# Seven block products in place of eight for the down-projection of two chunks

## The chip, the cores and the metric

The kernel runs on one core of one Trainium2 chip. The metric is the device time of one execution in microseconds, median of the runs; lower is better. All inputs start in HBM and the output ends there.

## The reference, cut to what matters

One layer of a hybrid block on 2048 tokens of width 1024, all in float32:

```
hn  = rms_norm(x, g_mix_pre);  [u | q | k | v] = hn @ w_in
mix = concat[pool_mixer(u), rms_norm_per_head(stick_breaking_attention(q, k, v))] @ w_out
h   = x + rms_norm(mix, g_mix_post)
m   = square(relu(rms_norm(h, g_mlp_pre) @ w_up)) @ w_down      # w_up 1024x4096, w_down 4096x1024
h   = h + rms_norm(m, g_mlp_post)
out = h + sigmoid(h @ w_ple_gate) * rms_norm(p @ w_ple_proj, g_ple)
```

The change is in `square(relu(...)) @ w_down`, in the sums of weights that it needs, and in constants that set the order of everything.

## The kernel before

**Tiling.** Tokens are taken in four chunks of 512 (`CH`), features in tiles of 128 (`P`). Float32 products are made from two halves: a number is split into a rounded high part and the rest (`split`: ScalarE copies the high part, VectorE subtracts), and `mm3` does three matmuls for each tile product (high by high, high by low, low by high), each 128x128 by 128x512. A `page` is an SBUF tile of 128x1024 float32 (512 KB); there are 53 of them (`PAGES`) for everything that moves, and 8 PSUM banks. Split weights are written to HBM at their first use (`dd["w_down"]`, `dd["w_up"]`, ...) and loaded again from there.

**Stages.** First the embeddings (`ple`), projections and attention of the chunks; the feed-forward of chunks 0 and 1 (`mlp_ups`, `mlp_downs`) is mixed with attention. Then chunks 2 and 3 together: `moving_up` builds seven sums and differences of the activations (28 pages, the tile `xs`), and 16 `up_pair` calls each make two of the 32 row tiles of the up-projection for both chunks from seven block products instead of eight (`block`, Winograd's form of Strassen's scheme), 84 matmuls each. The results, `relu` and square applied, are stored as `dd["m"]`. `gate(0)`, the gate of chunk 0, stands before the pairs. Then 8 calls of `down_pair` do the down-projection: each loads four row tiles of `m`, splits them for both chunks, loads four split weights, and for each chunk and each of 8 output tiles runs 4x3 matmuls into one bank, which is added into a running sum in SBUF (tile `acc`). Last come `mlp_post` for chunks 2 and 3 (sum of squares, norm, residual, store `h2`) and the gates of chunks 1, 2 and 3 (tiles `actg`, `gs`, `geh`), which load `h2` again.

**Order.** Nothing runs as written. Every operation is recorded with a time `plan.t` that only TensorE's work moves on; `deadlines` walks back from the users and gives each operation of the other engines the latest time at which it must run. `order` is a list scheduler with a model of the engines, the DMA queue and the pages, which takes the most urgent operation that is ready and fits; `issue` writes the instructions out in that order. So each engine has one fixed order, and every DMA is issued by SyncE's queue, in one fixed order too. The constants (`T_*`, `R_*`, `G_*`, `NORM_LAG`, `AHEAD`, `LEAD`, `EVICT`) shift the due times.

Of the kernel before, what the change touches and what calls it, by code (L numbers as in the profile page):

```python
# [13 lines left out]
F32 = mybir.dt.float32  # L14
# [19 lines left out]
GD = 4  # L34
# [20 lines left out]
G_OUT = 8  # L55
G_OUT2 = 3
G_OUT3 = 12
NORM_LAG = (34.149, 10.442)
# [76 lines left out]
class Op:  # L135
    __slots__ = ("engine", "dur", "calls", "deps", "outs", "allocs", "bufs", "prio", "seq", "place",
                 "left", "ready", "end")
# [14 lines left out]
MARGIN = 2.0  # L152
LATENCY = {
# [9 lines left out]
EVICT = -0.186  # L163
AHEAD = {'pe': 42.752, 'act': 24.695, 'dve': 39.763, 'pool': 25.085, 'sp': 42.237}
LEAD = {'pe': 3.156, 'act': 0.736, 'dve': 0.004, 'pool': 1.033, 'sp': 1.845}
# [31 lines left out]
class Plan:  # L197
# [3 lines left out]
    def __init__(self, tc, banks, pages):  # L201
# [10 lines left out]
        self.t, self.rate, self.bias = 0.0, 1.0, 0.0  # L212
# [23 lines left out]
    @contextmanager  # L236
    def early(self, lead):
        self.bias -= lead
        yield
        self.bias += lead  # L240

    def cost(self, name, method, out, kw, args):
# [11 lines left out]
        if name == "act":  # L254
            psum = all(a.buf.tag in BANKS for a in src if a.buf.tag)
            return (0.051 if psum else 0.093) + n / 1200.0 + (0.07 if len(out.steps) > 2 else 0.0)
        if name == "dve":
            scalars = any(isinstance(kw.get(k), Ref) for k in ("initial", "scalar"))
            if method == "tensor_tensor_scan":
                return 0.2 + n / 460.0  # L260
            return 0.072 + n / 960.0 + (0.058 if scalars else 0.0)
# [36 lines left out]
    def new(self, name, dur):  # L298
        op = Op()
        op.engine, op.dur, op.calls, op.deps, op.allocs, op.bufs = name, dur, [], set(), [], set()  # L300
        op.prio, op.seq, op.end = self.t + self.bias, None, None
# [25 lines left out]
    def deadlines(self):  # L327
# [5 lines left out]
        for op in reversed(self.ops):  # L333
# [4 lines left out]
            op.prio = min(op.prio, late) if e == "pe" else late  # L338
# [146 lines left out]
class Net:  # L485
# [430 lines left out]
    def mlp_ups(self, gi, acts, w_up, dd, first, tag):  # L916
        ms = [[] for _ in acts]
        for j in range(GF):
            unit = self.weight(w_up[gi * GF + j], dd["w_up"][gi * GF + j], first)
            rl = self.page("rl")  # L920
            for i in range(len(acts)):
# [4 lines left out]
                self.dve.tensor_tensor(out=r, in0=r, in1=r, op=ALU.mult)  # L926
# [4 lines left out]
    def moving(self, k, b11, b12, b21, b22):  # L931

        sub = lambda out, a, b: self.dve.tensor_tensor(out=out, in0=a, in1=b, op=ALU.subtract)
# [19 lines left out]
    def moving_up(self, c, d, rows):  # L953

        got = []
        for k2 in range(2):
            low, high = self.both(c, d, k2, rows), self.both(c, d, k2 + 2, rows)
            for j in range(2):
                got.append(self.moving(k2, low[0][:, j, :], low[1][:, j, :], high[0][:, j, :], high[1][:, j, :]))
# [65 lines left out]
    def up_pair(self, b, xs, w_up, dd):  # L1025
        def square(o, t, r):
            self.act.activation(r, r, AF.Relu)
            self.dve.tensor_tensor(out=r, in0=r, in1=r, op=ALU.mult)
# [5 lines left out]
    def down_pair(self, gi, accs, w_down, dd):  # L1034
        ms = [[], []]
        for j in range(GD):
            t = self.page("mi")
            self.sp.dma_start(out=t, in_=dd["m"][gi * GD + j])
            for i in range(2):
                ms[i].append(self.pair("m", t[:, i, :]))  # L1040
        units = [self.weight(w_down[gi * GD + j], dd["w_down"][gi * GD + j], False) for j in range(GD)]
        for i in range(2):
            for ot in range(NK):
                ps = self.bank("dw")
                cs = slice(ot * P, (ot + 1) * P)
                self.mm3(ps, [(units[j][0][:, cs], units[j][1][:, cs], ms[i][j][:, 0, :], ms[i][j][:, 1, :])
                              for j in range(GD)])
                if gi == 0:
                    if ot % 2 == 0:
                        accs[i].append(self.page("acc"))  # L1050
                    self.act.copy(accs[i][-1][:, ot % 2, :], ps)
                else:
                    a = accs[i][ot // 2][:, ot % 2, :]
                    self.dve.tensor_tensor(out=a, in0=a, in1=ps, op=ALU.add)
# [67 lines left out]
def build(tc, x, xr, p, gains, w_in, w_v, w_pool, w_out, w_up, w_down, w_gate, w_ple, out):  # L1122
    with (
# [22 lines left out]
        dd["m"] = [dram(f"m{f}", [P, 2, CH]) for f in range(NF)]  # L1146
        net.h1 = dd["h1"]
# [134 lines left out]
```

## Time and profile before

| | |
|---|---|
| device time, median of 3 runs | 2620.93 us (2620.6 to 2620.98) |
| the profiled execution: device time, span | 2619.36 us, 2617.6 us |
| TensorE matmul busy, granted clock | 2578.0 us (98%), 0.995 |
| VectorE, ScalarE, GpSimd busy | 1781.9 us (68%), 1070.2 us (41%), 683.4 us (26%) |
| DMA: share of 16 engines on the main queue, bytes, mean rate | 69.2%, 653.71 MB, 250 GB/s |

The span is the stretch from the first to the last instruction; 1.76 us of the profiled execution's time lie around it. Matmul busy time is modelled with overlap, so 98% says that TensorE was seldom without a matmul, not that it ran at its peak. Granted clock 1 is 2.4 GHz, 0.5 is 1.2 GHz.

### The profile page before, as it was taken

To read this page: it belongs to the slowest core of one execution; us is meant where nothing else is said; L and a number is where in the kernel's file an instruction comes from. 1 tells how busy PE (TensorE), PEld (TensorE's weight loads), DVE (VectorE), ACT (ScalarE), POOL (GpSimd) and SP (SyncE) were. 2 spreads that over 40 slices of the span, in tenths; PEclk is the share of its full clock that TensorE was granted. 3 is DMA by queue.
4 is the path that set the end of the run, shared out by engine and by line. 5 is a ranking of instruction groups with operands and counts; after the bars stand their busy time and mean duration, and the time that the engine had idled before them with its cause. 6 is when DMAs were issued, how large, how long until landed. Compare 5 with 4: busy or idle time off the path is not lost. (4 is left out here: it accounts for less than half of the span.)

```text
span 2617.6 us, 33833 instructions
## 1 busy us (share of the span) xinstructions
PE 2578.0 (98%) x12088; PEld 2106.5 (80%) x12088; DVE 1781.9 (68%) x2471; ACT 1070.2 (41%) x1999; POOL 683.4 (26%) x635
## 2 busy tenths in 40 slices
PE   8999999999999999999999999999999999999999
PEld 7888787887888888788888888887788888888877
DVE  7375858879888769997758775289856642334464
ACT  9344546646655456455444442134222331010221
POOL 0033536346533444443443541000000000000000
PEclk9999999999999999999999999999999999999999
DMA  9999787986767748774557546676855573432896
GB/s 390 369 354 341 255 300 262 313 297 231 283 239 258 251 156 340 264 273 165 193 169 265 210 150 252 223 307 246 296 201 186 191 299 137 153 137 98 316 359 260
DMA packets 211977, 653.71 MB, mean 250 GB/s; under 512 B 22752, under 2 KB 39136, under 8 KB 211808
## 3 DMA queue, kind: packets, MB, share of 16 engines
q1 hardware_dynamic: 211808, 651.54, 69.2%
q8 instruction: 96, 1.57, 0.2%
q14 instruction: 73, 0.60, 0.1%
HBM read 457.47 MB, written 193.99 MB: 249 GB/s over the span
## 5 line engine op out<-in xcount | busy, mean ns | idle before, releaser
L279 POOL TENSOR_TENSOR pr<-pr,q 128x511 f32<-128x511 f32 (+4 forms) x512 | 573.3, 1137 | 710.3 <-ACT pr L279 281.2
L279 PE MATMUL dw<-m,wh 128*128 128x512 f32 x2048 | 642.4, 395 | 0.0
L279 PE MATMUL dn<-act,wh 128*128 128x512 f32 x1792 | 577.6, 403 | 0.0
L279 DVE TENSOR_TENSOR_SCAN q<-q,ones 128x512 f32<-128x512 f32 (+1 forms) x320 | 405.7, 1284 | 66.1 <-ACT q L279 65.1
L279 PEld LDWEIGHTS dw<-m,wh 128*128 128x128 f32 x2048 | 375.5, 188 | 72.7 <-issue 0.7
L279 PE MATMUL dw<-m,wl 128*128 128x512 f32 x1024 | 399.7, 390 | 0.0
L279 DVE TENSOR_TENSOR acc<-acc,dw 128x512 f32<-128x512 f32 x352 | 237.7, 682 | 237.8 <-PE dw L279 236.8
L279 PEld LDWEIGHTS dn<-act,wh 128*128 128x128 f32 x1792 | 319.7, 190 | 57.9 <-issue 3.2
L279 PE MATMUL dn<-act,wl 128*128 128x512 f32 x896 | 351.9, 393 | 0.0
L279 POOL TENSOR_TENSOR ms<-ms,mhalf 128x4 f32<-128x4 f32 (+1 forms) x36 | 54.3, 1508 | 1046.9 <-DVE ms L279 1013.9
L279 ACT ACTIVATE q<-z 128x512 f32<-128x512 f32 (+1 forms) x320 | 173.2, 542 | 179.6 <-PE z L279 158.6
L279 ACT CAST at<-tp 128x512 fp32r<-128x512 f32 (+2 forms) x320 | 167.5, 530 | 186.6 <-PE tp L279 164.5
L279 PEld LDWEIGHTS dw<-m,wl 128*128 128x128 f32 x1024 | 192.2, 188 | 41.4
L279 DVE TENSOR_TENSOR at<-tp,at 128x512 fp32r<-128x512 f32 (+2 forms) x320 | 189.2, 597 | 48.7 <-ACT at L279 48.1
L279 PEld LDWEIGHTS dn<-act,wl 128*128 128x128 f32 x896 | 168.8, 188 | 37.4
L279 PE MATMUL op<-at,kv 128*128 128x512 f32 (+3 forms) x640 | 185.1, 369 | 8.0 <-DVE at L279 7.8
L279 PE MATMUL dn<-xs,so 128*128 128x512 f32 x768 | 191.8, 389 | 0.0
L279 PE MATMUL z<-kv,qd 128*128 128x512 f32 (+3 forms) x640 | 180.3, 366 | 4.3 <-DVE at L279 3.4
L279 ACT ACTIVATE pr<-z 128x512 f32<-128x512 f32 (+1 forms) x320 | 172.6, 541 | 5.9 <-POOL pr L279 3.1
L279 PE MATMUL tp<-ident,pr 128*128 128x128 f32 x1088 | 170.1, 272 | 2.1 <-DVE acc L279 1.3
L279 PEld LDWEIGHTS dn<-xs,so 128*128 128x128 f32 x768 | 144.1, 188 | 30.5 <-DVE so L279 0.5
L279 PEld LDWEIGHTS tp<-ident,pr 128*128 128x128 f32 x1088 | 135.6, 140 | 40.1 <-DVE acc L279 2.1
(145 smaller groups left out, 3611.0 us busy)
## 6 DMA issues: line engine op xcount, KB each, us to landing
ws<-in_w_up SPq DMA_DIRECT2D x64, 512.0 KB, 5.8
wh<-d_w_down SPq DMA_DIRECT2D x64, 512.0 KB, 5.7
wl<-d_w_down SPq DMA_DIRECT2D x64, 512.0 KB, 5.9
xin<-d_h SPq DMA_DIRECT2D x48, 512.0 KB, 8.3
wh<-d_w_up SPq DMA_DIRECT2D x48, 512.0 KB, 5.3
wl<-d_w_up SPq DMA_DIRECT2D x48, 512.0 KB, 5.5
kv<-d_k SPq DMA_DIRECT2D x80, 256.0 KB, 6.0
kv<-d_v SPq DMA_DIRECT2D x80, 256.0 KB, 6.3
```

The lines of the kernel that those rows point to most:

```text
L279: fn(*[a.real() if isinstance(a, Ref) else a for a in args], **{k: a.real() if isinstance(a, Ref) else a for k, a in kw.items()})
```

## The change

- **Down-projection.** `down_pair` now treats the four row tiles of a group as two pairs, each a 2x2 block problem (two halves of the inner dimension; two halves of the output blocks; two chunks). Per pair it makes four differences of `m` on **GpSimd** (`moving` takes the engine as an argument) and seven splits; three weight halves come from `dd["w_down"]`, four sums of weights from a new store `dd["sd"]`. Seven products times four output blocks, 2x3 matmuls each, go to one bank each and are added into **28 half pages of running sums, one for each product and block, over all 8 groups**. In the last group the loops are turned (output block outside, products inside), and after each block seven additions combine the sums into the outputs of both chunks.
- **Sums of weights.** `stationary_down` runs 16 times, once after each `up_pair`: it loads two raw row tiles of `w_down`, makes four sums on VectorE, splits them, and stores four pages in `dd["sd"]`. `within(SOON)` sets its due time to 15 us after the pair.
- **Squares.** In `mlp_ups` and `up_pair` the square after `relu` moves from VectorE (a product) to ScalarE (`Square`).
- **Rows early.** `prenorm` of chunks 2 and 3 is recorded inside the projection of the chunk before, at a time set back by `T_AHEAD`.
- **Planner.** Durations of ScalarE and VectorE are taken 1.1 times longer (`WEAR`); about twenty constants change, among them the pace of attention (`R_ATT`, `R_ATT2`) and the groups at which the output projections start.

The core of the diff:

```diff
-T_PRE = (12.427, 22.281)
-T_PLE = (0.0, 23.664, 52.404, 38.46)
+T_PRE = (5.628, 28.649)
+T_PLE = (0.0, 23.664, 43.677, 40.12)
-R_ATT = 3.117
+R_ATT = 3.632
+R_ATT2 = 3.024
+T_AHEAD = 30.179
-G_OUT = 8
-G_OUT2 = 3
-G_OUT3 = 12
-NORM_LAG = (34.149, 10.442)
+G_OUT = 4
+G_OUT2 = 1
+G_OUT3 = 11
+NORM_LAG = (39.625, 9.401)
+SOON = 15.0
+WEAR = 1.1
...
-EVICT = -0.186
-AHEAD = {'pe': 42.752, 'act': 24.695, 'dve': 39.763, 'pool': 25.085, 'sp': 42.237}
+EVICT = -0.384
+AHEAD = {'pe': 71.988, 'act': 28.302, 'dve': 36.362, 'pool': 22.185, 'sp': 42.237}
...
                 r = rl[:, i, :]
                 self.act.activation(r, ps, AF.Relu)
-                self.dve.tensor_tensor(out=r, in0=r, in1=r, op=ALU.mult)
+                self.act.activation(r, r, AF.Square)
...
+    def stationary_down(self, n, w_down, dd):
+        f = 4 * (n // 2) + n % 2
+        view = []
+        for i in (f, f + 2):
+            t = self.plan.tile([P, D], F32, "ws")
+            self.sp.dma_start(out=t, in_=w_down[i])
+            v = t.rearrange("p (b h c) -> p h b c", b=4, h=2)
+            view += [v[:, 0], v[:, 1]]
...
+        add(s1[1], a21, a22, ALU.add)
+        add(s2[1], s1[1], a11, ALU.subtract)
+        add(s3[1], a11, a21, ALU.subtract)
+        add(s4[1], a12, s2[1], ALU.subtract)
+        for d, t in zip(dd["sd"][n], (s4, s1, s2, s3)):
+            self.sp.dma_start(out=d, in_=self.pair("so", t[0]).as_(F32))
+
+    def down_pair(self, gi, accs, dd):
+        xs, ws = [], []
+        for j in range(2):
+            low, high = [self.page("mi") for _ in range(2)]
+            for t, f in ((low, 4 * gi + j), (high, 4 * gi + 2 + j)):
+                self.sp.dma_start(out=t, in_=dd["m"][f])
+            xs.append(self.moving(self.pool, low[:, 0, :], low[:, 1, :], high[:, 0, :], high[:, 1, :]))
+            kept = []
+            for f, h in ((4 * gi + j, 0), (4 * gi + 2 + j, 0), (4 * gi + 2 + j, 1)):
+                t = self.page("wa", F32R)
+                for part in range(2):
+                    d = dd["w_down"][f][part].rearrange("p (b h c) -> p h b c", b=4, h=2)[:, h]
+                    self.sp.dma_start(out=t[:, part, :].rearrange("p (b c) -> p b c", b=4).as_(F32), in_=d)
+                kept.append(t)
+            sums = []
+            for i in range(4):
+                t = self.page("wa", F32R)
+                self.sp.dma_start(out=t.as_(F32), in_=dd["sd"][2 * gi + j][i])
+                sums.append(t)
+            ws.append([kept[0], kept[1], sums[0], kept[2], sums[1], sums[2], sums[3]])
+        order = (0, 1, 2, 6, 4, 5, 3)
+        last = gi == NF // 4 - 1
+        steps = [(i, ob) for ob in range(4) for i in order] if last else [(i, ob) for i in order for ob in range(4)]
+        for i, ob in steps:
+            ps = self.bank("dw")
+            cs = slice(ob * P, (ob + 1) * P)
+            self.mm3(ps, [(ws[j][i][:, 0, cs], ws[j][i][:, 1, cs], xs[j][i][:, 0, :], xs[j][i][:, 1, :])
+                          for j in range(2)])
+            a = accs(i, ob)
+            if gi == 0:
+                self.act.copy(a, ps)
+            else:
+                self.dve.tensor_tensor(out=a, in0=a, in1=ps, op=ALU.add)
+            if last and i == order[-1]:
+                for into, of in ((1, 0), (5, 0), (6, 5), (5, 4), (4, 6), (2, 5), (3, 6)):
+                    self.dve.tensor_tensor(out=accs(into, ob), in0=accs(into, ob), in1=accs(of, ob), op=ALU.add)
...
         def project(c):
-            if c > 1:
-                acts[c] = net.prenorm(x[c], xr[c], G_PRE)
             net.in_proj(c, w_in, w_v, acts[c], dd)
+            if 0 < c < NCH - 1:
+                with plan.resumed(plan.t - T_AHEAD):
+                    acts[c + 1] = net.prenorm(x[c + 1], xr[c + 1], G_PRE)
             net.u_proj(c, w_in, acts[c], dd)
...
         for b in range(NF // 2):
             net.up_pair(b, xs, w_up, dd)
-        accs = [[], []]
-        for gi in range(NF // GD):
-            net.down_pair(gi, accs, w_down, dd)
+            with plan.within(SOON):
+                net.stationary_down(b, w_down, dd)
...
+        for gi in range(NF // 4):
+            net.down_pair(gi, sums, dd)
+        accs = [[held[c, ob] for ob in range(4)] for c in (2, 3)]
         net.mlp_post(2, accs[0], dd)
         net.mlp_post(3, accs[1], dd)
```

## Rows read from the trace of the kernel before

**Rows 1.** The page: span and busy time of each engine.

```profile
span 2617.6 us, 33833 instructions
...
PE 2578.0 (98%) x12088; PEld 2106.5 (80%) x12088; DVE 1781.9 (68%) x2471; ACT 1070.2 (41%) x1999; POOL 683.4 (26%) x635
```

**Rows 2.** Windows: bounds, length, busy (x) of PE, PEld, DVE, ACT, POOL, clock, DMA.

```profile
262.00:300.00 38.00, 31.63 (x145) 23.77 (x144) 35.76 (x56) 24.44 (x54) 22.60 (x16) 0.87 0.67 219
...
600.00:680.00 80.00, 74.42 (x359) 59.13 (x357) 75.73 (x81) 54.80 (x101) 51.68 (x38) 0.98 0.79 277
680.00:1766.00 1086.00, 1082.15 (x5238) 885.13 (x5238) 820.89 (x1048) 503.00 (x926) 403.66 (x359) 1.00 0.65 233
1766.00:1857.00 91.00, 86.29 (x376) 70.15 (x375) 85.25 (x138) 33.45 (x59) 1.40 (x1) 0.98 0.68 251
1857.00:2105.00 248.00, 248.00 (x1096) 205.43 (x1095) 162.79 (x261) 69.49 (x122) 0.00 (x0) 1.00 0.57 210
2124.40:2471.40 347.00, 347.00 (x1532) 287.43 (x1531) 127.25 (x196) 52.60 (x95) 0.00 (x0) 1.00 0.48 177
...
2516.00:2534.00 18.00, 15.23 (x56) 11.01 (x55) 14.81 (x24) 5.92 (x11) 0.00 (x0) 0.91 1.02 404
2534.00:2617.60 83.60, 77.67 (x343) 64.02 (x341) 41.54 (x64) 13.91 (x24) 0.00 (x0) 0.99 0.75 286
```

**Rows 3.** The tile dw in the down-projection of chunks 2 and 3.

```profile
L279 PE MATMUL dw<-m,wh x1024: 389/389/389, 2123.2 to 2472.3; 128*128 128x512 f32 x171
...
L279 PE MATMUL dw<-m,wl x512: 389/389/389, 2123.7 to 2472.5; 128*128 128x512 f32 x171
```

**Rows 4.** VectorE's groups over the span, count | busy us, mean ns.

```profile
L279 DVE TENSOR_TENSOR acc<-acc,dw 128x512 f32<-128x512 f32 x352 | 237.7, 682 | 237.8 <-PE dw L279 236.8
...
L279 DVE TENSOR_TENSOR rl<-rl 128x512 f32<-128x512 f32 x64 | 50.6, 790 | 52.7 <-ACT rl L279 52.5
L279 DVE TENSOR_TENSOR so<-sa,so 128x512 fp32r<-128x512 f32 x64 | 44.0, 689 | 8.5 <-ACT so L279 8.0
L279 DVE TENSOR_TENSOR mo<-mo 128x512 f32<-128x512 f32 x64 | 43.8, 689 | 6.9 <-ACT mo L279 6.8
...
L279 DVE SCALAR_TENSOR_TENSOR acc<-acc,gains,nrm 128x512 f32<-128x512 f32 x32 | 22.2, 749 | 3.5 <-ACT nrm L279 3.4
...
L279 DVE TENSOR_TENSOR xin<-xin,acc 128x512 f32<-128x512 f32 x32 | 20.4, 687 | 0.0
...
L279 DVE TENSOR_TENSOR ypool<-pt,ypool 128x512 fp32r<-128x512 f32 x16 | 17.8, 1111 | 4.3 <-ACT ypool L279 4.3
```

**Rows 5.** ScalarE's groups over the span, the same columns.

```profile
L279 ACT ACTIVATE mo<-mo 128x512 f32<-128x512 f32 x64 | 40.3, 633 | 185.9 <-DVE mo L279 100.9 <-issue 57.4 <-PE dn L279 24.1
...
L279 ACT CAST so<-sa 128x512 fp32r<-128x512 f32 x64 | 37.3, 615 | 3.5 <-DVE sa L279 2.6 <-DMA out<-geh 0.8
```

**Rows 6.** GpSimd's groups over the span, the same columns.

```profile
L279 POOL TENSOR_TENSOR pr<-pr,q 128x511 f32<-128x511 f32 x224 | 348.0, 1560 | 320.5 <-DVE q L279 160.6 <-ACT at L279 32.0 <-ACT pr L279 25.3
...
L279 POOL TENSOR_TENSOR pt<-u 128x527 f32<-128x527 f32 x16 | 20.5, 1281 | 67.0 <-ACT u L279 44.2 <-PE op L279 8.3 <-issue 8.1
```

**Rows 7.** Windows of 20 us where up pairs run, columns as in rows 2.

```profile
1860.00:1880.00 20.00, 20.00 (x90) 16.57 (x89) 17.24 (x30) 7.25 (x14) 0.00 (x0) 1.00 1.03 405
1880.00:1900.00 20.00, 20.00 (x90) 16.54 (x89) 13.58 (x22) 6.09 (x11) 0.00 (x0) 1.00 0.54 196
```

**Rows 8.** DMA issues: count, KB each, median us to landing.

```profile
mi<-d_m SPq DMA_DIRECT2D x32, 512.0 KB, 5.7
...
d_v<-ve SPq DMA_DIRECT2D x16, 512.0 KB, 6.6
```

**Rows 9.** SyncE's queue from 1840 to 2120 us: whom it waited for, times, longest.

```profile
SPq L279 <- DVE mo L279: 151.8, 30, 11.1
```

**Rows 10.** TensorE's waits over the span.

```profile
PE op L279 <- DVE at L279: 7.8, 8, 2.8
...
PE dn L279 <- DVE xs L279: 4.7, 1, 4.7
```

More of the change, by code (lines that the diff above doesn't have):

```diff
@@ L33 @@
 GF = 2
-GD = 4
 EPS = 1e-6
@@ L136 @@
     __slots__ = ("engine", "dur", "calls", "deps", "outs", "allocs", "bufs", "prio", "seq", "place",
-                 "left", "ready", "end")
+                 "left", "ready", "end", "by")
 class Engine:
@@ L234, in resumed, with within @@
         self.t = kept
+    @contextmanager
+    def within(self, time):
+        self.by = self.t + time
+        yield
+        self.by = None
     @contextmanager
@@ L255, in cost @@
             psum = all(a.buf.tag in BANKS for a in src if a.buf.tag)
-            return (0.051 if psum else 0.093) + n / 1200.0 + (0.07 if len(out.steps) > 2 else 0.0)
+            return WEAR * ((0.051 if psum else 0.093) + n / 1200.0 + (0.07 if len(out.steps) > 2 else 0.0))
         if name == "dve":
@@ L337, in deadlines @@
             late = min(need) - dur if need else op.prio + TAIL
-            op.prio = min(op.prio, late) if e == "pe" else late
+            op.prio = min(op.prio, late) if e == "pe" else late if op.by is None else min(late, op.by)
         for op in self.ops:
@@ L1032, in up_pair @@
             self.sp.dma_start(out=dd["m"][2 * b + o], in_=outs[o])
[L1034 to L1054, printed above, removed]
+    def stationary_down(self, n, w_down, dd):
[6 more added lines that the diff above has]
+            view += [v[:, 0], v[:, 1]]
+        a11, a21, a12, a22 = view
+        pages = [self.page("sa") for _ in range(2)]
+        s1, s2, s3, s4 = [(t[:, h, :], t[:, h, :].rearrange("p (b c) -> p b c", b=4)) for t in pages for h in range(2)]
+        add = lambda out, a, b, op: self.dve.tensor_tensor(out=out, in0=a, in1=b, op=op)
+        add(s1[1], a21, a22, ALU.add)
[4 more added lines that the diff above has]
+            self.sp.dma_start(out=d, in_=self.pair("so", t[0]).as_(F32))
@@ L1146, in build @@
         dd["m"] = [dram(f"m{f}", [P, 2, CH]) for f in range(NF)]
+        dd["sd"] = [[dram(f"sd{n}{i}", [P, 2, CH]) for i in range(4)] for n in range(NF // 2)]
         net.h1 = dd["h1"]
@@ L1205, in attend @@
             kept = plan.t, plan.rate
-            plan.at(t_att, R_ATT)
+            plan.at(t_att, R_ATT if c < 2 else R_ATT2)
             net.attention([(c, pair) for pair in range(4)], dd, 1)
@@ L1231, in build, with half, sums @@
             net.up_pair(b, xs, w_up, dd)
-        accs = [[], []]
-        for gi in range(NF // GD):
-            net.down_pair(gi, accs, w_down, dd)
+            with plan.within(SOON):
+                net.stationary_down(b, w_down, dd)
+        held = {}
+        def half(key):
+            if key not in held:
+                held[key] = net.page("acc")
+            return held[key]
+        def sums(i, ob):
+            key, h = {0: (("x", ob), 0), 5: (("x", ob), 1), 1: ((2, ob), 0), 3: ((2, ob), 1), 2: ((3, ob), 0),
+                      4: ((3, ob), 1), 6: (("y", ob // 2), ob % 2)}[i]
+            return half(key)[:, h, :]
+        for gi in range(NF // 4):
+            net.down_pair(gi, sums, dd)
+        accs = [[held[c, ob] for ob in range(4)] for c in (2, 3)]
         net.mlp_post(2, accs[0], dd)
```

18 lines of the change are left out of this document (9 added, 9 removed).

## The prediction, made before the changed kernel had run

> **What bounds the kernel now.** I read the page first, to see which engine is ever without work: TensorE is busy for 98% of the span, VectorE for 68% [rows 1]. A busy TensorE is a modelled figure, so the next view is the table of windows, cut at the borders of the stages; the reader is to look at the count of matmuls beside each length. In the down-projection of chunks 2 and 3 there is no gap: 1532 matmuls in 347.0 us, 0.2265 us each, at clock 1.00 [rows 2], and each matmul's record is the same 389 ns from first to last [rows 3]. So there a matmul left out is 0.2265 us won, as long as nothing else becomes late. The same table shows where something is late already: 262 to 300 us (TensorE 31.63 of 38 us, clock 0.87), 600 to 680 us (74.42 of 80), the start of the up pairs (86.29 of 91), and the start of chunk 2's gate near 2520 us (15.23 of 18, clock 0.91). In all of them VectorE is at 82 to 95% of the stretch [rows 2], and TensorE's waits name it: for `at` 7.8 us, for `xs` 4.7 us [rows 10]. So the bound is TensorE, with VectorE next, and a few seams where VectorE is late.
>
> **The products.** Before, the down-projection has 8 groups x 2 chunks x 8 output tiles x 4 row tiles x 3 = 1536 matmuls; after, 8 x 7 products x 4 blocks x 2 pairs x 3 = 1344. The 192 that go, at 0.2265 us, are **-43.5 us**. A group then takes 168 matmuls, 38.05 us.
>
> **VectorE in the down stage.** A group gets 28 additions from a bank at 0.682 us and 14 splits at 0.689 us [rows 4]: 28.7 us of 38.05, 75%, where it was 127.25 of 347, 37% [rows 2]. ScalarE has 14 copies at 0.615 us [rows 5], 8.6 us. GpSimd has 8 differences at 1.281 to 1.560 us [rows 6], 10.2 to 12.5 us, and was idle here. All three hide under TensorE; the price is 0 if no split is slowed much. The nearest row for a split slowed beside GpSimd is `ypool`, 1.111 us against 0.689 [rows 4]: 14 x 0.42 = 5.9 us more, 34.6 of 38.05, still hidden. I take 0.
>
> The Trainium skill speaks against this part: its page "SBUF — State Buffer", section "Who interferes with whom", says that a VectorE instruction with two SBUF inputs and a GpSimd instruction that reads SBUF cannot overlap, the later one blocks until the first is done. By that rule the sum would be worse than by the row; the rival below has it as a mechanism of this kernel.
>
> **DMA in the down stage.** A group loads 4 pages of `m`, 12 half pages of weights in 512 B pieces, and 8 pages of sums: 18 x 524,288 bytes = 9.44 MB in 38.05 us, 248 GB/s. The nearest transfers in such small pieces, the stores of `ve`, land in 6.6 us where `mi` lands in 5.7 [rows 8]; the engines move 405 GB/s when pressed [rows 7]. Hidden.
>
> **The up stage.** A pair is 84 matmuls, 19.03 us. VectorE has 162.79 of 248 us there [rows 2], 12.5 us a pair; four squares go (4 x 0.689, `mo`), four sums and four splits come (8 x 0.689): 15.3 of 19.03. ScalarE: 69.49 of 248 is 5.3 us a pair, with 4 x 0.633 and 4 x 0.615 [rows 4, 5] it is 10.3. DMA is the tight one. A pair moves 7 page-sized amounts now (two raw tiles, two split pages, two halves, two stores of `mo`); `stationary_down` adds two loads and four stores, so 13 x 524,288 bytes = 6.82 MB in 19.03 us, 358 GB/s. The mix of loads and stores around 1870 us went at 405 GB/s with the engines full [rows 7], which makes it 16.8 us of 19.03; scaled from the stage's own 210 GB/s at share 0.57 [rows 2] it is 18.5 us. Both fit, barely. What is queued behind is SyncE's one order: a store of `so` waits for VectorE, and the next pair's weights stand behind it. At the start, where VectorE had 85.25 of 91 us [rows 2], the eight new operations less four squares are 2.8 us more work in front of the late `xs`. I take **+2**, from 0 up to the rival below.
>
> The page "HBM Reference", section "Specifications (TRN2)", of the Trainium skill gives about 358 GB/s for a core whose pair streams too; by that figure a pair's transfers would take as long as its matmuls and any wait would show. The 405 GB/s of [rows 7] decide here.
>
> **Pages at the seams.** Before, the last group holds 8 pages of sums, 8 of `m` and 8 of weights, and leaves 29 of 53. After, the 28 half sums are 14 pages, and a turned last group holds all 28 pages of its operands until its last block: 42, which leaves 11. So 18 pages fewer, 18 x 524,288 bytes at 405 GB/s = 23 us of transfers, can be fetched ahead for the gates. The last 83.6 us have a DMA share of 0.75 [rows 2], 21 us of room, which takes most of that. The last group's own 28 pages must come while the group before still holds its own. I take **+3** for both seams (into the last group, out of it), from 0 to 12, half of the 23.
>
> **The end.** Before, chunk 2 was finished half a group ahead of chunk 3. After, both are ready only after the last block, and chunk 2's norm, residual, store, load and split must pass under gate 1, 192 matmuls or 43.5 us. VectorE's work from the start of the last group to the start of gate 2: 28 additions from banks (19.1 us), 28 combinations (19.3, priced like `so`), 14 additions of squares (9.6), the residual's 8 x 0.749 + 8 x 0.687 (11.5), 16 splits of `actg` for chunks 1 and 2 (11.0) and gate 1's own 24 operations (16.5, at 0.689) [rows 4]: 87 us in 38.05 + 43.5 = 81.5. About 7 of the 87 can wait (chunk 3's squares, gate 1's last tiles), so it just fits, with no room for the chain of a norm between them. That seam already cost 2.8 us of idle and 9% of 18 us of clock, 4.4 us, with VectorE at 14.81 of 18 [rows 2]. I take **+7** beyond that; at least 0, and at most 28.9 if combinations and squares (19.3 + 9.6) all stand behind the last product.
>
> **The squares of chunks 0 and 1.** 64 squares at 0.790 us leave VectorE [rows 4], 50.6 us, in stretches where it is at 76 to 95%; ScalarE takes 64 x 0.633 = 40.5 us and is at 503.0 of 1086 [rows 2, 5], so it hides them. What TensorE loses in those stretches is 6.4 us of idle and 13% of 38 us of clock from 262 to 300, 5.6 and 2% of 80 from 600 to 680, and 3.9 until 1766 [rows 2]: 22 us. The first of them has no squares near it, it is chunk 1's rows and attention at once; the earlier rows and the new due times move that work, by an order that I cannot read from here. I take **-5**, between -22 (all gone) and +22 (as many new ones).
>
> **The sum.** 2619.36 (the profiled execution: span 2617.6 and 1.76 around it) - 43.5 + 2 + 3 + 7 - 5 = 2582.9; that execution is 1.57 below the median of the three runs, so 2584.5. A measurement here tells a change of 0.2%, 5.2 us, from none.
>
> **The rivals.**
>
> *VectorE late at the end.* The 87 us above are late by their full overhang: the chain of combinations, squares, norm and residual is serial, and TensorE is idle before gate 2 for 20 to 29 us with its clock halved behind it. For it: VectorE ended the wait there before. Against: gate 1's operations can be ordered behind. Of 28.9 us, 7 are in the sum: +22, 2606. Chance 0.13.
>
> *GpSimd blocks VectorE in the down stage.* If each of the 8 differences of a group holds up VectorE for its whole length, VectorE needs 28.7 + 12.5 = 41.2 us for 38.05, +3.1 us in each of 8 groups, 25 us: 2610. For it: `ypool` at 1.111 us. Against: its 0.42 us are far from a whole GpSimd operation, and two thirds of VectorE's operations here read a bank. Chance 0.06. (That is what the rule of the Trainium skill quoted above would do here.)
>
> *The stalls before 1766 us vanish.* Squares, rows and new due times together clear the 22 us: 17 more than taken, 2567; with a smoother end 2563. Against: a new order also makes new ones. Chance 0.09.
>
> *SyncE's queue starves the up pairs* (the one that ends slower). SyncE waited 151.8 us for `mo` in some 15 pairs [rows 9], 10 us a pair, and loads behind a waiting store do not start. With 16.8 us of transfers a pair has 2.2 us to spare. If 4.9 of the 10 us leave the DMA engines empty, a pair takes 21.7 us, 16 x 2.7 = 43.5 us, and the whole gain is gone; from there on the kernel is slower. With 6 us it is 16 x 3.8 = 61, 2645. For it: today the same waits leave half of the DMA time unused. Against: with much queued the engines stayed full in [rows 7], and `stationary_down` has its results due 15 us late, not at once. Chance 0.09, of which 0.01 lands within 0.2%.
>
> **How the numbers follow.** The sum has 0.63. Faster: 0.63 + 0.09 + 0.11 of the late end + 0.05 of GpSimd = 0.88; same: 0.02 + 0.01 + 0.01 = 0.04; slower: 0.08. The range, 2562 to 2612, takes in the cleared stalls, the late end and GpSimd at their prices, and leaves out the starved queue (0.09) and about as much again for two dear seams at once or new stalls in attention.
>
> **What would show it.** The down stage: 1344 matmuls on `dw` in about 304.5 us, no wait of TensorE for `xs`, `wa` or `acc`. The up pairs: still 19.0 us apart, DMA share 0.9 or more, VectorE about 80%. GpSimd: 64 differences between 1.3 and 1.6 us, splits beside them under 1.2. The end: a wait before gate 2 of some 10 us, for `actg`. Before 1766 us: fewer than 22 us lost. The prediction is wrong if pairs stand further apart than 19.0 us (the queue), if `acc` holds banks in the down stage (VectorE), if TensorE waits at the change of stages for pages, or if attention, in its new order, loses more than it did.

## The result, and the profile after

The changed kernel takes **2585.6 us** (median of 4 runs, 2584.08 to 2585.78) beside 2620.76 us (2620.29 to 2620.98) for the one before, a ratio of 0.9865 [0.9853, 0.9877]: 35 us faster, forecast 2584.5. The profiled execution took 2585.55 us. The page of the changed kernel:

```profile
span 2583.8 us, 34478 instructions
...
PE 2534.3 (98%) x11896; PEld 2070.5 (80%) x11896; DVE 1881.0 (73%) x2631; ACT 1220.8 (47%) x2251; POOL 766.2 (30%) x699
```

TensorE's busy time fell by 43.7 us and its share stayed 98%, so the page says nothing of where the other 10 us went. Cutting both traces at the same instructions does (lengths in us, from the start of one matmul to the start of the other):

| stretch | before | after | change | forecast |
|---|---|---|---|---|
| to gate 0 (embeddings, attention, chunks 0 and 1) | 1766.6 | 1757.0 | -9.6 | -5 |
| gate 0 to up pair 4 | 128.8 | 133.0 | +4.2 | +2, with the line below |
| up pair 4 to the last up matmul | 228.9 | 230.3 | +1.4 | |
| to gate 1 (the down-projection) | 347.0 | 304.1 | -42.9 | -43.5 |
| gate 1 to the end | 146.2 | 159.4 | +13.2 | +7, and +3 for pages at both seams |

At the borders the matmuls of neighbouring stages are mixed. The changed kernel runs 9 matmuls of the down-projection before the last up matmul, the one before ran 3; and the one before ran 3 of them after the start of gate 1, the changed kernel none. At 0.2265 us each, six matmuls are the whole +1.4 of the third line. Counted by work and not by cuts, the up stage lost 4.2 us, the down-projection won 42.3 and the end lost 13.8.

The windows of the changed kernel, with the columns of [rows 2], answer to the rows shown of before:

```profile
262.00:300.00 38.00, 35.23 (x189) 27.75 (x188) 36.83 (x56) 24.73 (x57) 25.35 (x17) 1.00 0.87 301
600.00:680.00 80.00, 78.91 (x393) 63.92 (x392) 69.91 (x83) 56.56 (x103) 45.94 (x40) 1.00 0.83 304
680.00:1757.00 1077.00, 1072.05 (x5200) 878.68 (x5199) 777.58 (x992) 540.60 (x996) 404.16 (x370) 1.00 0.66 232
1800.00:1860.00 60.00, 54.42 (x217) 40.03 (x216) 57.40 (x94) 32.00 (x57) 0.00 (x0) 0.97 0.69 252
1890.00:2100.00 210.00, 210.00 (x928) 173.87 (x928) 155.53 (x255) 106.46 (x187) 0.00 (x0) 1.00 0.97 358
2124.40:2424.20 299.80, 298.86 (x1318) 247.48 (x1319) 233.68 (x337) 88.04 (x151) 83.61 (x57) 1.00 0.87 293
2385.00:2424.00 39.00, 39.00 (x174) 32.29 (x173) 37.29 (x61) 10.02 (x17) 0.00 (x0) 1.00 0.70 261
2424.00:2470.00 46.00, 46.00 (x211) 37.76 (x210) 38.98 (x66) 12.05 (x20) 2.47 (x2) 1.00 1.03 410
2470.00:2490.00 20.00, 5.18 (x13) 3.01 (x12) 19.69 (x35) 4.61 (x8) 0.37 (x1) 0.61 1.03 417
2500.00:2583.80 83.80, 76.43 (x338) 62.97 (x336) 35.74 (x56) 13.22 (x24) 0.00 (x0) 0.98 0.66 250
```

Read them from the middle. The down stage is nearly as forecast, TensorE full at clock 1.00 with VectorE at 78%. The up pairs fit: DMA share 0.97 at 358 GB/s, with TensorE full. The two stalls of before at 262 and 600 us are smaller. The loss is in two places: 1800 to 1860, where VectorE has 57.40 of 60 us, and 2470 to 2490, where TensorE has 13 matmuls in 20 us and its clock falls to 0.61. The second is the largest stall of the whole trace. The timeline around it, on TensorE, then SyncE, ScalarE and VectorE (start, length, instruction, count, and in brackets the idle time before it with what ended it; `nm` is the bank of a norm, `dn` here a bank of a gate, `d_h` the rows in HBM):

```profile
2474.40 0.79 PE L289 MATMUL nm<-rt,sel 8*128 8x512 f32 x1 [2.84 <-DVE rt L289]
2483.84 0.79 PE L289 MATMUL dn<-actg,wh 128*128 128x512 f32 x1 [8.64 <-ACT actg L289]
2487.52 0.80 PE L289 MATMUL dn<-actg,wh 128*128 128x512 f32 x1 [2.89 <-DVE actg L289]
...
2456.78 0.32 SPq L289 DMA_DIRECT2D d_h<-xin  x1
...
2473.23 0.33 SPq L289 DMA_DIRECT2D xin<-d_h  x1
...
2483.17 1.14 ACT L289 CAST actg<-xin 128x512 fp32r<-128x512 f32 x2 [7.29 <-DMA xin<-d_h]
...
2476.68 5.37 DVE L289 SCALAR_TENSOR_TENSOR acc<-acc,gains,nrm 128x512 f32<-128x512 f32 x8
2481.98 4.88 DVE L289 TENSOR_TENSOR xin<-xin,acc 128x512 f32<-128x512 f32 x8
2486.79 2.48 DVE L289 TENSOR_TENSOR actg<-xin,actg 128x512 fp32r<-128x512 f32 x4
```

Behind 2.84 us for chunk 3's norm TensorE waits for ScalarE's high half of chunk 2's rows, and ScalarE waits 7.29 us for their load from HBM; then for VectorE's split, which stands behind the residual of chunk 3 in VectorE's fixed order. Chunk 2's own residual had been done by 2462.8. What lies between is the store of these rows to `h2`, first issued at 2456.78, and the load back, first issued at 2473.23. The DMA view from 2450 to 2495 us (issues, count, KB each, median us to landing) shows what such a trip costs there:

```profile
DMA packets 5109, 18.63 MB, mean 414 GB/s; under 512 B 567, under 2 KB 567, under 8 KB 5106
...
xin<-d_h SPq DMA_DIRECT2D x9, 512.0 KB, 9.9
d_h<-xin SPq DMA_DIRECT2D x8, 512.0 KB, 9.4
```

The queue is full at 414 GB/s. A page lands some 10 us after its issue, once out and once back, and its issue has to come up in SyncE's order each time.

### The profile page after: what moved, and what is told of

The parts are those of the page before. It is cut to its first block, busy times and chain, and to the rows that moved or that the text cites. A ratio compares the mean times of both kernels' runs of the same rounds, so it can differ in the third digit from the quotient of the medians.

```text
span 2583.8 us, 34478 instructions
## 1 busy us (share of the span) xinstructions
PE 2534.3 (98%) x11896; PEld 2070.5 (80%) x11896; DVE 1881.0 (73%) x2631; ACT 1220.8 (47%) x2251; POOL 766.2 (30%) x699
## 4 chain that ended last, share of the span: by engine, by line
PE 90%; DVE 5%; DMA 3%; issue 0%; ACT 0%; SPq 0%; DVEq 0%; POOL 0%; POOLq 0%
PE dn L289 49%; PE dw L289 24%; PE z L289 5%; PE op L289 5%; PE tp L289 4%; DVE q L289 2%; PE pl L289 2%; PE nm L289 2%; DMA xin<-d_h 1%; DMA wh<-d_w_gate 0%; DMA wl<-d_w_gate 0%; DVE acc L289 0%; DVE xin L289 0%; DVE at L289 0%; DMA wl<-d_w_in 0%
## 5 line engine op out<-in xcount | busy, mean ns | idle before, releaser
L289 POOL TENSOR_TENSOR pr<-pr,q 128x1 f32<-128x1 f32 (+4 forms) x512 | 556.1, 1103 | 666.2 <-ACT pr L289 277.3
L289 DVE TENSOR_TENSOR acc<-acc,dw 128x512 f32<-128x512 f32 x436 | 292.9, 682 | 104.7 <-PE dw L289 98.6
L289 PEld LDWEIGHTS dn<-act,wh 128*128 128x128 f32 x1792 | 316.2, 189 | 54.7 <-issue 2.7
L289 PE MATMUL dw<-m,wh 128*128 128x512 f32 x1024 | 326.9, 400 | 1.8 <-DVE acc L289 1.8
L289 PE MATMUL dw<-xs,wa 128*128 128x512 f32 x1344 | 305.6, 389 | 1.0 <-DVE xs L289 1.0
L289 PEld LDWEIGHTS dw<-xs,wa 128*128 128x128 f32 x1344 | 252.2, 188 | 53.7 <-DVE xs L289 1.4
L289 ACT CAST at<-tp 128x512 fp32r<-128x512 f32 (+3 forms) x320 | 167.0, 527 | 171.3 <-PE tp L289 145.6
L289 PEld LDWEIGHTS dw<-m,wh 128*128 128x128 f32 x1024 | 184.7, 189 | 36.9 <-DVE acc L289 2.3
L289 PE MATMUL dw<-m,wl 128*128 128x512 f32 x512 | 200.9, 392 | 0.0
L289 POOL TENSOR_TENSOR ms<-ms,mhalf 128x4 f32<-128x4 f32 (+1 forms) x36 | 55.6, 1545 | 465.6 <-DVE ms L289 453.0
L289 POOL TENSOR_TENSOR xt<-mi 128x512 f32<-128x512 f32 x32 | 47.9, 1497 | 474.9 <-PE dn L289 304.3
```

The costliest lines, as they stand in the source:

```text
L289: fn(*[a.real() if isinstance(a, Ref) else a for a in args], **{k: a.real() if isinstance(a, Ref) else a for k, a in kw.items()})
```

## The experiments

Each expectation names its own theories. The runs are told by what they are about: the end (E1, E2, E4, E10), the up stage and its queue (E3, E9, E8), the time before gate 0 (E5, E6), the differences (E7), and variants of the best version (E11, E12). A time without a range is from one run and stands beside the 2585.55 us of the profiled changed kernel; stage lengths are cut as in the table. Kernels that are edited only behind gate 0 start it anywhere from 1754.1 to 1757.2 us, so for a single run a difference of some 3 us in the whole time tells nothing, and the stages are read.

**E1. Chunk 2's and 3's rows are split where they are made.** Gates 2 and 3 take them from SBUF, with no load back.

```diff
                 self.dve.tensor_tensor(out=t[:, j, :], in0=t[:, j, :], in1=ys[2 * i + j], op=ALU.add)
+                if acts is not None:
+                    acts.append(self.pair("actg", t[:, j, :]))
...
-        net.mlp_post(2, accs[0], dd)
+        post[2] = net.mlp_post(2, accs[0], dd)
...
-            net.gate((c,), [net.gate_acts(c, dd)], w_gate, dd, out, c == 0)
+            net.gate((c,), [post[c] if c in post else net.gate_acts(c, dd)], w_gate, dd, out, c == 0)
```

> Edit: the rows of chunks 2 and 3 after the residual are split for their gates from SBUF, where the residual left them, and not after a store to HBM and a load back (the store stays, since the gate still adds the rows at its end). Theory A, the round trip: the TensorE gap before gate 2 (16.2 us without a matmul between 2471 and 2488 us, clock at half for 17 us) is the way of chunk 2's rows through a full DMA queue; without it the gap falls under 4 us and the kernel takes 2568 to 2577 us. Theory B, VectorE's load: the gap comes from 28 combinations and the sums of squares that VectorE has in hand at the end; then it stays above 12 us and the time is 2582 to 2589 us.

Measured, median of 4 runs: 2566.49 us (2565.87 to 2567.37), ratio to before 0.9793 [0.9776, 0.9809], 19 us less than the changed kernel, and 1.5 under the span of theory A. From gate 1 to the second output tile of gate 2 it takes 52.7 us where the changed kernel takes 70.2. The window of the stall, and TensorE's only wait between 2424 and 2500:

```profile
2470.00:2490.00 20.00, 19.71 (x85) 15.03 (x84) 20.00 (x35) 5.17 (x9) 0.68 (x1) 1.00 1.02 405
```

```profile
PE dn L289 <- DVE actg L289: 0.2, 1, 0.2
```

VectorE is as full as in the changed kernel (20.00 of 20) and TensorE does not wait for it. Without the trip there is no stall.

**E2. No combinations** (left out: the 28 additions that make outputs of the products).

```diff
-            if last and i == order[-1]:
+            if False:
```

> Edit: the 28 additions that combine the running sums after the last group are left out, so the output is not the reference's. Theory A, the round trip: the gap before gate 2 stays at 10 us or more, because the rows still go to HBM and back behind the gates' loads; 2580 to 2587 us. Theory B, VectorE's load: 19.3 us of VectorE's 87 us go, the gap falls under 6 us; 2568 to 2577 us.

Measured: 2582.24 us. VectorE's work between 2424 and 2470 fell from 38.98 to 26.03 us, and the stall stayed, as the round trip's theory had it, 66.6 us from gate 1 to the second tile of gate 2:

```profile
2424.00:2470.00 46.00, 46.00 (x211) 37.74 (x210) 26.03 (x47) 7.62 (x13) 2.40 (x2) 1.00 1.03 411
2470.00:2490.00 20.00, 8.45 (x26) 5.92 (x25) 17.80 (x30) 4.61 (x8) 0.00 (x0) 0.66 1.02 390
```

So VectorE's load, which the prediction had named for the end, is not the stall. It is worth at most the 3.6 us by which this stretch is shorter than in the changed kernel: in six runs whose edits leave the end as it is (E3, E5, E6, E7, E8, E9) it takes from 67.5 to 72.0 us.

**E4. The last group is not turned** (products outside, output blocks inside, as in the other groups).

```diff
-        steps = [(i, ob) for ob in range(4) for i in order] if last else [(i, ob) for i in order for ob in range(4)]
+        steps = [(i, ob) for i in order for ob in range(4)]
```

> Edit: the last group of the down-projection goes product by product like the others, and the combinations of all four blocks come after its last product. Pages then come free all through the group, and loads for the gates can start some 25 us earlier, but 28 combinations (19.3 us) stand behind the last product. Theory A, the round trip through a full queue: the queue is emptier, but the rows start later; about 2585 to 2595 us. Theory B, VectorE's load: the gap grows by 10 us or more, 2595 to 2605 us. If held pages alone made the gap (a third theory), it shrinks by 8 us or more: 2577 us or less.

Measured: 2570.28 us. The trip is still there and the stall is nearly gone, 55.6 us: the theory of the held pages had it right, and the one of the trip alone expected the opposite. The last group's own window shows how:

```profile
2385.00:2424.00 39.00, 39.00 (x174) 32.31 (x173) 37.99 (x63) 9.39 (x17) 0.00 (x0) 1.00 0.98 362
```

Pages come free during the last group, and the gates' loads are fetched there, 362 GB/s for 261 with the turned loop: (362 - 261) x 39 us = 3.9 MB, some 7 pages that need not go through the queue together with chunk 2's rows. The rate while these rows are stored, and the median landing of the stores from 2450 to 2495 us (9.4 in the changed kernel), show it:

```profile
2450.00:2460.00 10.00, 10.00 (x44) 8.13 (x44) 9.79 (x16) 1.78 (x3) 0.00 (x0) 1.00 0.92 313
...
d_h<-xin SPq DMA_DIRECT2D x8, 512.0 KB, 6.0
```

In the changed kernel those ten microseconds have 409 GB/s. ScalarE starts its first copy of the rows at 2470.6 and not 2483.2. So trip and held pages make the stall together: the trip is dear because the queue is full, and the queue is full because the turned group gives no page back until its last block.

**E10. Both at once**, E1 and E4.

> Edit: rows of chunks 2 and 3 split from SBUF (as in the first experiment) and the last group not turned (as in the fourth). Both remove the same gap, so the gains do not add: 2561 to 2568 us. If they removed different losses (the trip, and pages held), 2555 us or less.

Measured, median of 4 runs: 2566.22 us (2564.87 to 2567.34), ratio 0.9793 [0.9778, 0.9807], and 52.7 us for the same stretch. The gains do not add: it is one stall with two conditions.

**E3. No sums of weights** (left out: `stationary_down`; `wa` is loaded from `dd["m"]` in place of `dd["sd"]`, so that the down stage moves as much).

```diff
-            with plan.within(SOON):
-                net.stationary_down(b, w_down, dd)
...
-                self.sp.dma_start(out=t.as_(F32), in_=dd["sd"][2 * gi + j][i])
+                self.sp.dma_start(out=t.as_(F32), in_=dd["m"][4 * gi + i])
```

> Edit: the sums of weights are left out (two loads, eight VectorE operations, four splits' copies and four stores per up pair); the down-projection loads pages of m in their place, so the output is not the reference's. If the sums cost what the stage from gate 0 to the last pair lost against before (4.2 us, in the first three pairs, where VectorE is full), the time falls by 2 to 6 us, to 2579 to 2584 us, and pairs stand 19.0 us apart as before. If SyncE's queue were near starving the pairs, more than 8 us would come back, 2577 us or less. If they are free, 2584 to 2587 us.

Measured: 2576.03 us, 9.5 less. By the time alone this is the starved queue, more than 8 us; by stages it is not. 1.7 of the 9.5 are before gate 0, where nothing was changed. Gate 0 to pair 4 fell by 5.3 us: that is what the sums cost in the up stage. The rest of the pairs fell by 2.0, but only because no matmul of the down-projection stands before the last up matmul here, and 9 do in the changed kernel. The other 2.5 are 1.2 in the down-projection, counted by work, and 1.3 behind it.

```profile
1800.00:1860.00 60.00, 58.07 (x240) 45.07 (x239) 52.66 (x87) 28.47 (x51) 0.00 (x0) 0.97 0.74 267
1890.00:2100.00 210.00, 210.00 (x929) 173.87 (x928) 108.03 (x168) 85.46 (x150) 4.79 (x3) 1.00 0.55 195
```

In the first pairs VectorE drops from 57.40 to 52.66 us and TensorE does 240 matmuls for 217. TensorE's waits from 1757 to 1890 us in the changed kernel name VectorE for 4.7 us and transfers for 0.7:

```profile
PE dn L289 <- DVE so L289: 2.6, 1, 2.6
PE dn L289 <- DVE xs L289: 2.1, 4, 1.1
```

Without the sums the wait for `so`, a split of weights for the third pair, is gone. From pair 4 on DMA falls from 358 to 195 GB/s and VectorE from 155.53 to 108.03 us, and the pairs stay 19.0 us apart: in the steady pairs the sums are hidden.

**E9. Sums due later** (`SOON = 15.0` to `80.0`), to take them out of the first pairs.

> Edit: the sums of weights are due 80 us after their pair and not 15. Theory A: they cost what VectorE lacks between 1800 and 1860 us, where it is 95% busy with the activations' sums, gate 0 and the first sums of weights; done some pairs later they are hidden, the fifth pair begins at 1883 to 1887 us (1890.1 in the changed kernel, 1883.0 without the sums), and the time is 2579 to 2583 us, if the gap before gate 2 stays. Theory B, their transfers cost it: the same transfers come later, in a stage whose DMA share is 0.97, and the pairs there stretch; 2584 us or more.

Measured: 2586.63 us. Gate 0 to pair 4 fell by 6.2 us and the pairs stayed 19.04 us apart, as theory A had it, but the whole time came out on theory B's side: the down stage took 316.2 us, 12.1 more, of which 1.4 are six matmuls more on its side of the border. Its start here, and the same stretch of the changed kernel:

```profile
2120.00:2210.00 90.00, 83.08 (x345) 66.40 (x344) 71.53 (x98) 39.59 (x69) 26.96 (x18) 0.96 1.04 372
```

```profile
2120.00:2210.00 90.00, 89.03 (x393) 73.40 (x392) 62.77 (x88) 42.09 (x74) 29.71 (x20) 1.00 1.06 364
```

The late sums run into the first groups of the down-projection, where DMA is full (1.04) and VectorE is needed for the splits. A piece of the chain that ended last (start, us, what) shows a weight load that is issued only behind two of the late sums (`sa`):

```profile
2192.96 1.22 DVE sa L289 x2
2194.18 0.24 SPq L289
2194.42 0.05 issue
2194.47 7.83 DMA wa<-d_w_down
```

**E8. Two of the four sums stored twice.** 15 page transfers a pair instead of 13, to see how near the queue is to its end.

```diff
-            self.sp.dma_start(out=d, in_=self.pair("so", t[0]).as_(F32))
+            so = self.pair("so", t[0])
+            self.sp.dma_start(out=d, in_=so.as_(F32))
+            if len(more) < 2:
+                more.append(dd["sx"][n][len(more)])
+                self.sp.dma_start(out=more[-1], in_=so.as_(F32))
```

> Edit: each call for the sums of weights stores two of its four pages a second time, to other places in HBM that nobody reads: 15 page-sized transfers in a pair and not 13, 7.86 MB. If the engines move 405 to 413 GB/s in the pairs, that is 19.0 to 19.4 us for 19.03 us of matmuls: the pairs stretch by 0 to 0.4 us, 2585 to 2593 us in all. If they move only what the share before implied (18.5 us for 13), it is 21.3 us a pair: 16 x 2.3 us more, 2610 to 2625 us. If SyncE's order is what limits them, more than that.

Measured: 2595.5 us, 9.9 more, 2.5 over the span of the first theory and far under the second.

```profile
1890.00:2100.00 210.00, 209.59 (x922) 172.20 (x921) 155.90 (x254) 109.38 (x187) 0.00 (x0) 1.00 1.03 414
```

The pairs are 19.04 to 19.8 us apart (231.2 us from pair 4 to the end, 0.9 more, and 2.3 more counted by work), and the backlog is paid at the start of the down stage, which takes 313.7 us with a wait of 5.0 us for `wa` from `dd["sd"]`. So the engines move 414 GB/s here, 16% more than the 358 of the changed kernel, and with that they are full.

**E5. Squares back on VectorE** in `mlp_ups`, chunks 0 and 1.

```diff
-                self.act.activation(r, r, AF.Square)
+                self.dve.tensor_tensor(out=r, in0=r, in1=r, op=ALU.mult)
```

> Edit: the 64 squares of chunks 0 and 1 go back to VectorE (the changed kernel otherwise). Theory A: 50.6 us more of VectorE in the attention stages cost TensorE some of the 9.6 us that the changed kernel gained before gate 0; the stretch up to gate 0 grows from 1757.0 us to 1762 us or more, the time to 2589 to 2600 us. Theory B, the order alone made that gain: gate 0 begins within 3 us of 1757.0, 2583 to 2588 us.

Measured: 2586.92 us, gate 0 at 1759.4 and not 1757.0. In the runs whose edit lies behind gate 0 it starts anywhere from 1754.1 to 1757.2, so 2.4 us are at the edge of what this can tell. Theory B's bounds held; the squares are a part of the 9.6 at most, 2.3 to 5.4 us by that spread.

**E6. The planner's constants of before** (`T_PRE`, `T_PLE`, `R_ATT`, `G_OUT`, `NORM_LAG`, `EVICT`, `AHEAD`, `LEAD`, and `WEAR = 1.0`); rows early and squares stay.

> Edit: the changed kernel with the planner's constants of before (due times of the embeddings and rows, pace of attention, groups of the output projections, lags, looking ahead, and durations not lengthened); products, sums, squares on ScalarE and early rows stay. Theory A, the squares and early rows made the gain before gate 0: gate 0 begins at 1755 to 1760 us and the time is within 5 us of 2585.6. Theory B, the order made it: gate 0 begins at 1763 us or later, and the time is 2592 us or more.

Measured: 2582.67 us. Gate 0 starts at 1761.7, between the bounds of the two theories and 4.7 later than in the changed kernel, so the constants made about half of the 9.6. The time of the whole does not show it: pair 4 starts at 1891.0 us beside 1890.1, because the stretch from gate 0 to it is 3.7 us shorter, and the stretch from gate 1 to the end is 3.3 shorter. Why the first of these is shorter is not shown. It is no rule that time won before gate 0 is given back: in E10 and E7, whose edits lie behind the pairs, gate 0 starts 2.9 and 2.4 us earlier than in the changed kernel and pair 4 as much, 2.8 and 2.2 us.

**E7. The differences on VectorE** (`self.moving(self.dve, ...)` in `down_pair`).

> Edit: the 64 differences of m in the down-projection run on VectorE and not on GpSimd. If GpSimd's reads held up VectorE (the rival of the prediction), VectorE's own 64 x 0.69 us come in place of longer waits, the splits in the down stage fall back to 0.69 us, and the time stays or falls, 2580 to 2586 us. If they did not, VectorE goes from 28.7 to 34.2 us in a group of 38.05, still hidden: 2584 to 2588 us, the down stage within 1 us of 304.1. Only if VectorE were at its limit there would it grow, 2590 us or more.

Measured: 2583.35 us, 2.2 less, and gate 0 starts 2.4 us earlier, so the edit gained nothing that can be told. The down stage takes 304.2 us as before the edit, 1.2 less counted by work: the changed kernel's one wait in it, 1.0 us for `xs`, is gone. The splits, in the changed kernel and then here, in groups by form (count | busy us, mean ns of one):

```profile
L289 DVE TENSOR_TENSOR acc<-acc,dw 128x512 f32<-128x512 f32 x161 | 107.3, 684 | 43.5 <-PE dw L289 41.3
L289 DVE TENSOR_TENSOR xs<-mi,xs 128x512 fp32r<-128x512 f32 x37 | 41.1, 1134 | 3.0 <-ACT xs L289 3.0
L289 POOL TENSOR_TENSOR xt<-mi,xt 128x512 f32<-128x512 f32 x27 | 40.5, 1524 | 3.4 <-DMA mi<-d_m 3.1
L289 POOL TENSOR_TENSOR xt<-mi 128x512 f32<-128x512 f32 x25 | 37.8, 1513 | 137.8 <-PE dw L289 51.3 <-DMA wa<-d_w_down 30.8 <-DVE xs L289 26.4
L289 DVE TENSOR_TENSOR xs<-xt,xs 128x512 fp32r<-128x512 f32 x47 | 33.7, 745 | 0.0
```

```profile
L289 DVE TENSOR_TENSOR xs<-xt,xs 128x512 fp32r<-128x512 f32 x49 | 32.3, 686 | 0.0
L289 DVE TENSOR_TENSOR xs<-mi,xs 128x512 fp32r<-128x512 f32 x36 | 23.7, 686 | 0.3 <-ACT xs L289 0.3
```

The splits fell back to 0.69 us, as the theory of the held VectorE had it. The trace of the changed kernel, one instruction at a time, shows how GpSimd holds them up:

```profile
2358.61 2.39 DVE L289 TENSOR_TENSOR xs<-xt,xs 128x512 fp32r<-128x512 f32 x2
2358.73 1.71 POOL L289 TENSOR_TENSOR xt<-mi 128x512 f32<-128x512 f32 x1 [14.13 <-DVE acc L289]
...
2363.48 1.30 POOL L289 TENSOR_TENSOR xt<-mi,xt 128x512 f32<-128x512 f32 x1
2364.05 1.27 DVE L289 TENSOR_TENSOR xs<-xt,xs 128x512 fp32r<-128x512 f32 x1
```

The last split begins 0.57 us into a difference that ends at 2364.78, and ends 0.54 us after it; a split alone takes 0.68. So it is with all 22 splits that begin 0.4 us or more into a running difference: each ends 0.54 to 0.56 us after it, and takes 1.01 to 1.79 us. The other way round, a difference that begins beside a running split (the first pair of lines) ends 1.14 to 1.16 us after it and takes up to 1.76 us, where one alone takes 1.29 to 1.30, and a split that was first keeps its 0.69. The later of the two waits for the end of the first. In all the splits lose some 20 us in 8 groups, which is hidden under TensorE but for 1 us at most.

**E11 and E12. The best version with later sums**: E10 with `SOON = 80.0`, and that with the constants of E6.

> Edit: as the run before, and the sums of weights due 80 us after their pair. If the loss in the first pairs is VectorE's and apart from the end, it adds: 3 to 6 us less than the run before, 2556 to 2564 us. If sums that come later collide with the transfers of the down stage, no gain or a loss.

> Edit: as the run before, with the planner's constants of before. If what those constants give before gate 0 (4.7 us) is lost again by the fifth pair, as in the sixth experiment, the time is within 3 us of the run before. If late sums leave VectorE room in the first pairs, an earlier gate 0 counts in full, and this one is 4 to 6 us slower.

Measured, medians of 4 runs each: 2571.79 us (2570.33 to 2572.43), ratio 0.9813 [0.9799, 0.9828], and 2582.04 us (2581.31 to 2583.87), ratio 0.9856 [0.9839, 0.9872]. The first expectation fell: the shift from the first pairs (-5.5 us against E10) into the down stage (317.4 us, +14.0, of which 2.7 are twelve matmuls more on its side of the borders) costs 5.6 in all, also without the stall at the end. The second fell too, on the far side of both its theories, 10.3 us slower: against E11 gate 0 starts 5.4 later, the stretch to pair 4 is 2.0 longer and the rest of pairs and down stage 2.3, so that here nothing gives back the time before gate 0.

The best of all are E1 and E10 at 2566 us, 54 us under the kernel before and 19 under the changed one.

## Why the prediction was right, and where its steps were not

**The number.** Forecast 2584.5, measured 2585.6. The forecast change of the span was -36.5 us and the trace has -33.8; the 2.7 between are, counted by work, +2.2 in the up stage, +1.2 for the products and +3.8 for seams and end, less 4.6 before gate 0. That the sum came within 1.1 us is luck: costs that were put too low met a gain that was put too low as well, and the largest cost had another cause than the one named.

**The products: right.** The view of the tile `xs`, which the changed kernel has in place of [rows 3], has the 1344 matmuls, and TensorE waits once in the stage, 1.0 us for `xs`:

```profile
L289 PE MATMUL dw<-xs,wa x1344: 388/389/497, 2116.5 to 2424.2; 128*128 128x512 f32 x192
```

304.1 us between the cuts beside the 304.5 named, and 42.3 of 43.5 won, counted by work. The price of nothing for VectorE and DMA held but for that 1.0 us, with VectorE at 78% where 75% was worked out (for every group alike, though the first group's additions are ScalarE's copies). The slowed splits are in it: those of `mi` took 1.134 us on average, where 1.111 of `ypool` was the nearest row [rows 4]. GpSimd's own mean was 1.51 to 1.52 us, its waits for splits included. The rival of the blocked VectorE came in its mechanism and not in its price: E7's trace lines show splits held until the difference beside them ends, but the 57 additions from a bank that overlap a difference took 0.683 us, as the others did, and the loss is some 20 us in 8 groups, 2.6 a group, where the rival had 12.5. The rule of the Trainium skill, "SBUF — State Buffer", "Who interferes with whom", that a VectorE operation with two inputs in SBUF and a GpSimd operation that reads SBUF exclude each other, is what the trace shows, with the addition that reads a bank left free. The prediction read `ypool`'s mean as a slowing by 0.42 us and took it against the rule; a mean over splits of which some wait and some do not cannot tell these apart.

**The up stage: mechanism right, size wrong.** +2 was the term, +4.2 measured, and E3 puts all that the sums do there at 5.3. What the step had missed is that VectorE, at 96% from 1800 to 1860, is late for more than the first operations: it charged 2.8 us once, for one pair's eight operations, and the third pair, 23.9 us long where before it took 19.0, waits 2.6 us for a split on VectorE, a wait that E3 does not have. In the steady pairs the working was exact, 358 GB/s worked out and measured. Of the two ways to say how full the engines are with that, the scaling from the stage's own row, 18.5 of 19.03 us (0.97), is the share that the view shows, but the room is the one by the 405 GB/s of [rows 7], 0.88: E8 went at 414 GB/s, of which 358 are 0.86. The starved queue did not come: SyncE's wait for VectorE's `mo` went from 151.8 us [rows 9] to 10.7 between 1840 and 2120 (its longest in all is now 90.6 us for TensorE's `dn`), and pairs stayed 19.04 us apart from the fourth on. That rival also set the end of the gain at 43.5 us, the products' term alone; the whole forecast gain was 36.4, so 2.3 us a pair would have been enough. The figure of the Trainium skill, "HBM Reference", "Specifications (TRN2)", some 358 GB/s for a core whose pair streams too, was no ceiling for one core by itself, which the same section puts well above it: 414 GB/s for 210 us in E8.

**The end: wrong cause, size too small.** The term was +7, from 87 us of VectorE in 81.5; measured, with the seams' +3, +13.8 by work, and E2 shows that without the 28 combinations the stretch is 3.6 us shorter, little beyond the scatter, of the 17.5 that E1 wins. The step that failed is the sentence that the store and load of chunk 2's rows must pass under gate 1: it was listed and given no price. The trace of before had the trip at this seam, with TensorE waiting 2.8 us for `actg`, but the stores landed in 5.0 us there (2495 to 2540 us):

```profile
d_h<-xin SPq DMA_DIRECT2D x8, 512.0 KB, 5.0
```

In the changed kernel they took 9.4. At 414 GB/s a page takes 524,288 / 414e3 = 1.27 us of the engines, and with some eight on the way it lands 10 us after its issue, two such trips in a row and a place in SyncE's order between. The part on pages had the other half of the cause, 18 pages fewer and 23 us of transfers that move behind the seam, and priced it by itself at +3, as if only its bytes mattered; E4 and E10 show that these bytes cost by the latency that they give to the rows. The clock's part is small. It fell behind the first of the three idle stretches (2.84, 8.64 and 2.89 us), and the first matmuls of gate 2 run at 1.2 GHz:

```profile
2470.00:2474.40 4.40, 1.11 (x5) 0.44 (x3) 4.09 (x10) 0.60 (x1) 0.37 (x1) 0.99 1.02 417
2474.40:2490.00 15.60, 4.07 (x8) 2.57 (x9) 15.60 (x26) 4.01 (x7) 0.00 (x0) 0.50 1.03 417
2484.00:2490.00 6.00, 3.11 (x7) 2.12 (x8) 6.00 (x11) 2.59 (x5) 0.00 (x0) 0.50 1.03 415
2490.00:2500.00 10.00, 10.00 (x43) 8.20 (x42) 5.40 (x9) 1.52 (x3) 0.00 (x0) 0.93 1.02 414
```

From 2487.5 to 2490 and for another 0.07 x 10 / 0.5 = 1.4 us they go at half speed, 3.9 us, of which half, 2 us, is lost.

**Before gate 0: better than the term, cause only half settled.** -9.6 for -5, within its bounds. E6 gives 4.7 to the constants, E5 2.4 to the squares, with a scatter of 3 us among kernels that are the same up to there. The rows built early, and `WEAR` apart from the other constants, were not tried by themselves. In E6, 3.7 of the 4.7 us come back before pair 4, in E12 none of its 5.4, so what this stretch is worth in the whole time stays open.

**The other rivals.** VectorE late at the end, 2606: the stall came where it said, from something else, and at half its price. The cleared stalls: a part of them came (262 to 300: 2.8 us of idle for 6.4, no clock lost), but not the 2567.

## What to carry to other kernels

A store and a load back between two steps is priced by the state of the queue at that moment, not by its bytes: look for who fills the queue there, and which held buffers made those loads late. Time won in one stretch may or may not reach the next border (pair 4 here: it did in E10, hardly in E6), so read an edit there too, and count the matmuls on either side of a border before its lengths are compared. A mean over operations of which some wait and some do not hides the rule: look at them one by one. A due time moved to relieve one stage has to be followed into the stage that it is moved to: 80 us of slack took 6 us off one and put 12 on the other.

## What the runs showed of the hardware

One core moved 405 to 417 GB/s of mixed loads and stores for stretches of 20 to 210 us, and at that rate a 512 KB page landed some 10 us after its issue, where the changed kernel's median for `mi` is 6.0. GpSimd's subtraction of two 128x512 float32 operands took 1.29 to 1.30 us alone. A VectorE subtraction with both inputs in SBUF that began while it ran ended 0.54 to 0.56 us after it (0.68 us alone, up to 1.79 so), and GpSimd's waited in the same way when it came second; an addition on VectorE with one input in a bank took 0.68 us beside it or not. After 2.84 us of idle time TensorE's granted clock fell from 0.99 (2470 to 2474.4 us) to 0.50; after two further idle stretches, of 8.64 and 2.89 us, it did 3.9 us of matmuls at 1.2 GHz and had 2.4 GHz again.
